# A two-layer hybrid encoder on one core: another order of the weight chunks, and wider matmuls in the up projection

## The chip, the core and the metric

The kernel runs on one core of one Trainium2 chip. The time is device microseconds of that core for one execution of the whole program; of several executions the median is taken. Five engines work beside each other, each through its own queue of instructions in a fixed order: TensorE (PE in the profile, its weight loads PEld), VectorE (DVE), ScalarE (ACT), GpSimd (POOL) and SyncE (SP, which here only issues transfers). An instruction that waits for another engine holds up all that stand behind it in its own queue.

## The reference

Input x is 256 rows of 1024 numbers, float32. Two layers are run. Each has a token-mixing part with three branches and a channel-mixing part:

```python
h = rms_norm(x, norm_mix_pre[i])
u_hy, q, k, v, g_out, gate_lr, u_pool, gate_logits = split(h @ w_in[i])
y_hy   = x0 * (fft_convolution(x1 * v_hy, filter) + bias * x1 * v_hy)  # x0, x1, v_hy: convolved thirds of u_hy
y_gla  = gated_linear_attention(q, k, v, g_out, gate_lr)              # 4 heads, both directions, chunks of 64 rows
y_pool = centred_mean_minus_self(u_pool, windows 2, 4, 8, 16) @ pool_w
gates  = sigmoid(gate_logits)                                         # 3 x 1024
merged = gates0 * (y_hy @ w_br_hyena) + gates1 * (y_gla @ w_br_gla) + gates2 * (y_pool @ w_br_pool)
x = x + rms_norm(merged @ w_out[i])
h = rms_norm(x, norm_ffn_pre[i])
a, b = split(h @ ffn_w_up[i], 2816)
x = x + rms_norm((gelu(dwconv3(a)) * b) @ ffn_w_down[i])
```

The decays of the attention are running sums of `max(log_sigmoid(gate) / 16, -1)` and enter as `exp` of them, so that logarithm, exponential, sigmoid, sine (in the filter) and GELU are all looked up in tables of ScalarE.

## The kernel before, in words

**Chunks.** All large weights of a layer are cut into 71 chunks of 128 x 2048 float32 (1 MB each), which SP fetches one after the other into three `raw` buffers. A chunk is then split into a high part in the matmul's reduced format (`split_upper`, line 205: one ACT copy of each half, 128 x 1024) and the low remainder (`split_lower`, line 222: one DVE subtraction of each half). Activations are kept as a high and a low part too. A product is three matmuls: high by high, high by low, low by high. Two ways to multiply are in use. In `chunk_x_stationary` (line 552) the activations are loaded as the stationary operand and 512 columns of weights move. In `ftile` (line 570) 128 columns of weights are stationary and the 256 rows of x move; `two_ftiles` (line 576) does so for the two halves of a 256-column chunk, with both results in one PSUM bank, and hands the bank to a function `post`.

**Order.** `CHUNK_ORDER` (line 47) says in which order the chunks are fetched, split and used. Its numbers, in words: 0 to 3 values and output gates of the attention; 4 to 9 the three inputs of the convolution (x1 and v first, then x0); 10, 11 queries; 12, 13 keys; 14, 15 inputs of the pooling; 16 to 21 sigmoid gates and projection of the convolution's branch (16, 17, 19, 20 gates, 18 and 21 projection); 22 to 27 the same for pooling; 28 to 33 for the attention; then output projection, up projection, down projection. A small chunk `lr` (the low-rank gate of the attention's decays) is put in after the fourth. In the kernel before, the order is values and gates, `lr` and decays, x1, v, x0, queries, pooling inputs, keys, and then the three branches (pooling, convolution, attention), each as gates and projection, half by half.

**Work beside the chunks.** `unit` (line 320) records the matmuls of a chunk and then lets side work go one step (`tick`) and splits later chunks ahead (`filler`), as far as `ahead["chunks"]` and the free buffers allow. Side work is written as generators: the convolution's filter (`filt`), the convolution (`hyena`), the pooling (`pool_pair`), the decays (`decay_gate`, four heads: two matmuls, two Exp on ACT, a minimum on DVE, one Ln on ACT, two scans on DVE, eight Exp of 128 x 128 on ACT), and the attention (`gla_head`). `post` of a query or key chunk multiplies the bank by the decays (`qk_post`, line 751), so that the bank stays taken until the decays are there. The program's own buffers are 37 slots of 4 KB per partition (`big`), 9 of 2 KB (`sml`) and 8 PSUM banks (`psm`); a slot goes to the next user in the order in which slots were given back.

**Who sets the order of instructions.** A scheduler that runs when the program is built puts the recorded instructions of each engine into their final order; the kernel steers it by the order of recording. Functions that need a table of ACT (Sin, Exp, Ln, Sigmoid, Gelu) keep their recorded order among themselves. Where two neighbours of these need different tables, a table load is put in front of the second. In the kernel before, `decay_all` (line 714) loads the set that has both logarithm and exponential, and all four heads run before the next sigmoid.

**Up projection.** For each of 11 pairs (order `UP_ORDER`), chunk a goes through `two_ftiles` and `a_post` (a three-tap convolution: one ACT and two DVE instructions for each 128 columns, then GELU); for 7 of the pairs chunk b goes through `two_ftiles` and `b_post`. That is 18 chunks of this kind a layer.

Of the kernel before, what the change touches and what calls it, by code (L numbers as in the profile page):

```python
# [18 lines left out]
P = 128  # L19
# [27 lines left out]
CHUNK_ORDER = (*range(12), 14, 15, 12, 13, *range(22, 28), *range(16, 22), *range(28, NCHUNK))  # L47
# [37 lines left out]
def trunk(ctx: ExitStack, tc: tile.TileContext, a: dict, out: bass.AP):  # L85
# [5 lines left out]
    big = Slots(spool, "b", 37, 4096)  # L91
# [3 lines left out]
    def f32(ap):  # L95
        return ap.bitcast(F32)
# [452 lines left out]
    def xt_alloc():  # L549
        return ([big.get([P, 4, L], F32R) for _ in range(2)], [big.get([P, 4, L], F32R) for _ in range(2)])  # L550
# [19 lines left out]
    def ftile(n, xt, f, o, width=256, kn=8):  # L570
        xth, xtl = xt
# [4 lines left out]
    def two_ftiles(n, xt, post):  # L576
# [14 lines left out]
    def layer(i, xt, chains):  # L591
# [13 lines left out]
        gw2 = big.get([P, DM])  # L605
        nc.gpsimd.dma_start(gw2[:], a["gw2"][i])
# [32 lines left out]


        nl = pos_of[("lr", i)]
        lrt = sml.get([P, L], F32R)
        pslr = psm.get([P, L])

        def fin_lr():
            act(lrt[:], pslr[:])
            tt(lrt[96:P, :], pslr[96:P, :], f32(lrt[96:P, :]), ALU.subtract)
            psm.put(pslr)

        def pe_lr():  # L650
            for k in range(8):
                w = wh[nl][0][:, k].rearrange("p a c -> p (a c)")
                for m in range(2):
                    mm(pslr[:], w, xt[m][k // 4][:, k % 4, :], k == 0 and m == 0, k == 7 and m == 1)

        ahead.update(chunks=3, reserve=0)
        unit([nl], pe_lr, fin_lr, cost=1.8, free=nl)
        g2 = room([P, DM], F32R)
        act(g2[:], gw2[:])
        tt(g2[32:64, :], gw2[32:64, :], f32(g2[32:64, :]), ALU.subtract)  # L660
        big.put(gw2)

        eb = [big.get([P, 2, 2, L]) for _ in range(2)]
        enb = [big.get([P, 2, 2, L]) for _ in range(2)]


        ebl = sml.get([P, 4, 3, 4])

        def rev(ap2):
            return bass.AP(ap2.tensor, ap2.offset + L - 1, [list(ap2.ap[0]), [-1, L]])  # L670

        ngb = cpool.tile([P, 8], F32, tag="ngb", name="ngb")
        nc.vector.tensor_scalar_mul(ngb[:], vec[:, i * NVEC + V_GB:i * NVEC + V_GB + 8], -1.0)

# [833 lines left out]
```

## Time and profile before

| | |
|---|---|
| median of 3 runs | 885.04 us (884.83 to 885.62) |
| the profiled execution's own time | 884.6 us |
| its span in the profile | 882.8 us |
| TensorE busy | 872.6 us, 99% |
| VectorE busy | 636.0 us, 72% |
| ScalarE busy | 512.4 us, 58% |
| table loads on ScalarE | 11, of 1283 ns each |
| mean granted clock of TensorE | 0.996 |

The 1.8 us between the profiled execution's time and its span lie outside of the first and the last instruction. A matmul's duration in the profile counts from its start to its last result, and the matmuls overlap; what one of them costs in a stream is the busy time of a group divided by its count. Layer 0 fills roughly the first 460 us of the span. Its mixing part ends at about 254 us, its up projection runs from about 265 to 392 us and its down projection follows. In the views, L120, L111, L106 and L114 are the lines of small helpers (matmul, DVE tensor-tensor, ACT, DVE scalar-tensor-tensor), so groups are told apart by tiles and shapes. Tile names are `b` for a 4 KB slot, `s` for a 2 KB slot, `p` for a PSUM bank, `raw` for a fetched chunk.

### The profile page before, as it was taken

How to read it: one execution, taken by the hardware profiler on the slowest of the kernel's cores; microseconds unless marked ns; L12 is line 12 of the kernel's file. 1: busy time of each engine (PE TensorE's matmuls, PEld its weight loads, DVE VectorE, ACT ScalarE, POOL GpSimd, SP SyncE). 2: the span in 40 equal slices, each digit the busy share in tenths (PEclk: the TensorE clock that was granted, in tenths of full speed). 3: DMA queues.
4: the chain of work that ended last, by engine and by line, in shares of the span. 5: the costliest groups of instructions: out<-in, count | busy, mean ns of one | idle time of the engine just before them, and what ended most of it. 6: DMA issues, size and time to landing. Idle time of an engine off the chain costs nothing.

```text
span 882.8 us, 13499 instructions
## 1 busy us (share of the span) xinstructions
PE 872.6 (99%) x5381; PEld 783.1 (89%) x5381; DVE 636.0 (72%) x925; ACT 512.4 (58%) x809; POOL 37.4 (4%) x86
## 2 busy tenths in 40 slices
PE   9999999999999999999999999999999999999997
PEld 7899987888888999998889999888888899999885
DVE  7899988766586798665288989876755967776612
ACT  7779666555365776554268865864543665555501
POOL 3000100000010000000010000000000000000000
PEclk9999999999999999999999999999999999999999
DMA  9854535746546446466349453465752674445501
GB/s 319 336 192 170 168 105 190 241 144 238 191 163 244 143 136 246 149 222 226 120 136 338 175 160 131 153 198 177 279 184 81 236 284 143 166 173 199 204 1 48
DMA packets 48431, 163.46 MB, mean 185 GB/s; under 512 B 3442, under 2 KB 29189, under 8 KB 33520
## 3 DMA queue, kind: packets, MB, share of 16 engines
q1 hardware_dynamic: 44352, 151.69, 49.2%
q0 software_dynamic: 4000, 10.90, 3.9%
q8 instruction: 42, 0.69, 0.3%
q14 instruction: 21, 0.17, 0.1%
q10 hardware_dynamic: 16, 0.00, 0.0%
HBM read 161.54 MB, written 1.05 MB: 184 GB/s over the span
## 4 chain that ended last, share of the span: by engine, by line
PE 96%; DVE 2%; DMA 1%; ACT 0%; issue 0%; SPq 0%; DVEq 0%; POOLq 0%; POOL 0%; ACTq 0%
PE p L120 94%; DVE b L111 1%; DMA raw<-in_wts 1%; PE p L374 1%; PE p L1059 0%; PE p L1204 0%; DMA x<-in_x 0%; ACT b L106 0%; PE p L775 0%; PE p L876 0%; PE p L1021 0%; DVE b L114 0%; DVE b L1281 0%; DVE s L111 0%; PE p L1294 0%
## 5 line engine op out<-in xcount | busy, mean ns | idle before, releaser
L120 PE MATMUL p<-b,b 128*128 128x256 f32 (+2 forms) x5022 | 842.1, 328 | 2.6 <-DVE b L111 1.9
L120 PEld LDWEIGHTS p<-b,b 128*128 128x128 f32 x5022 | 740.9, 190 | 85.6 <-DVE b L111 3.4
L111 DVE TENSOR_TENSOR b<-raw,b 128x1024 fp32r<-128x1024 f32 (+2 forms) x288 | 342.2, 1208 | 112.7 <-ACT b L106 55.2
L106 ACT ACTIVATE b<-raw 128x1024 fp32r<-128x1024 f32 (+2 forms) x290 | 292.0, 1041 | 159.3 <-PE p L120 128.3
L111 DVE TENSOR_TENSOR b<-p,b 128x512 f32<-128x512 f32 (+2 forms) x72 | 45.7, 654 | 66.5 <-ACT s L106 44.6
L106 ACT ACTIVATE b<-p 128x512 f32<-128x512 f32 (+3 forms) x90 | 50.1, 571 | 66.0 <-PE p L120 39.6
L106 ACT ACTIVATE s<-p 128x256 f32<-128x256 f32 (+3 forms) x50 | 20.3, 415 | 69.0 <-PE p L120 68.7
L114 DVE SCALAR_TENSOR_TENSOR s<-p,vec,s 128x255 f32<-128x255 f32 x104 | 49.3, 478 | 6.4 <-ACT s L106 5.5
L106 ACT ACTIVATE s<-p,vec 128x256 f32<-128x256 f32 x52 | 28.8, 558 | 19.0 <-DVE s L114 15.4
L106 ACT ACTIVATE s<-s 128x512 f32<-128x512 f32 (+6 forms) x54 | 29.0, 537 | 11.1 <-DVE s L111 5.6
L111 DVE TENSOR_TENSOR b<-s,b 128x512 fp32r<-128x512 f32 (+1 forms) x42 | 28.5, 685 | 6.0 <-ACT b L106 6.0
L106 ACT ACTIVATE b<-s 128x512 fp32r<-128x512 f32 x38 | 23.5, 625 | 9.6 <-DVE s L111 9.5
L111 DVE TENSOR_TENSOR b<-b,b 128x512 f32<-128x512 f32 (+4 forms) x28 | 22.4, 802 | 3.8 <-ACT b L106 3.3
L111 DVE TENSOR_TENSOR b<-b,p 128x512 f32<-128x512 f32 x24 | 16.2, 684 | 8.9 <-PE p L120 8.5
L111 DVE TENSOR_TENSOR s<-s,p 128x512 f32<-128x512 f32 x22 | 15.0, 683 | 8.1 <-ACT s L106 7.7
L106 ACT ACTIVATE b<-b,s 128x128 f32<-128x128 f32 x64 | 20.5, 395 | 0.0
L114 DVE SCALAR_TENSOR_TENSOR b<-p,vec,b 128x255 f32<-128x255 f32 (+1 forms) x40 | 19.1, 477 | 0.4 <-ACT b L106 0.3
L387 POOL TENSOR_TENSOR rstd<-mse,mhalf 128x1 f32<-128x1 f32 x16 | 8.9, 557 | 208.0 <-DVE mse L117 208.0
L106 ACT ACTIVATE b<-p,vec 128x256 f32<-128x256 f32 (+1 forms) x24 | 12.7, 530 | 8.1 <-PE p L120 5.8
L106 ACT ACTIVATE b<-b 1x512 f32<-1x512 f32 (+3 forms) x16 | 12.4, 780 | 4.1 <-DVE b L111 4.1
L106 ACT ACTIVATE s<-x 128x512 f32<-128x512 f32 x12 | 7.6, 633 | 11.6 <-DVE x L114 11.4
L164 POOL DMA_DIRECT2D b<-in_gains x7 | 3.9, 553 | 235.0 <-PE p L120 123.2
(108 smaller groups left out, 319.0 us busy)
## 6 DMA issues: line engine op xcount, KB each, us to landing
raw<-in_wts SPq DMA_DIRECT2D x116, 1024.0 KB, 4.9
raw<-in_wts SPq DMA_DIRECT2D x50, 512.0 KB, 4.7
b<-in_gains POOLq DMA_DIRECT2D x7, 512.0 KB, 4.9
b<-in_dft POOLq DMA_DIRECT2D x4, 512.0 KB, 5.4
raw<-in_wts SPq DMA_DIRECT2D x4, 256.0 KB, 5.4
b<-in_gw POOLq DMA_DIRECT2D x2, 512.0 KB, 6.1
b<-in_fw POOLq DMA_DIRECT2D x2, 512.0 KB, 7.3
b<-in_decay POOLq DMA_DIRECT2D x2, 512.0 KB, 7.6
```

Of the source, the lines that this page charges most:

```text
L106: ins = nc.scalar.activation(o, i, func, **kw)
L111: nc.vector.tensor_tensor(out=o, in0=x, in1=y, op=op)
L114: nc.vector.scalar_tensor_tensor(out=o, in0=x, scalar=s, in1=y, op0=op0, op1=op1)
L120: ins = nc.tensor.matmul(o, w, x, start=start, stop=stop).ins
L164: eng.dma_start(g[:], bass.AP(src.tensor, src.offset + (i * 4 + j) * DM, [[0, P], [1, DM]]))
L374: nc.tensor.transpose(ps[k // 4][:, k % 4, :], h[:, k * P:(k + 1) * P], ident[:])
L387: nc.gpsimd.tensor_tensor(out=r[:], in0=e[:], in1=mhalf[:, 0:1], op=ALU.pow)
```

## The change

Two things change. First, the chunks of the mixing part come in another order, and with it the parts of the program: values and gates, x1, v, x0, pooling inputs, the pooling branch (gates and projection), `lr`, then the decays beside the gates of the convolution's branch, queries and keys, the projection of the convolution's branch, and last the gates and the projection of the attention's branch. `branch` is cut into `gates` and `project`; the gates of a branch are held in buffers until its projection. How far splits run ahead of use changes too: 5 chunks with 3 slots kept in reserve where the convolution's inputs start, against 3 and 0 before.

Second, the high and the low part of an activation tile stand next to each other in memory (two fixed tiles for a layer's input in place of four `big` slots, of which there are now 33). In the up projection one matmul then moves 512 columns, 256 of the high and 256 of the low part, past the high weights; a second moves the 256 high columns past the low weights. Each 128 columns of output take a whole PSUM bank, whose two halves are added afterwards (one ACT copy, one DVE addition), and `post` reads the sum from a 2 KB slot.

```diff
-CHUNK_ORDER = (*range(12), 14, 15, 12, 13, *range(22, 28), *range(16, 22), *range(28, NCHUNK))
+CHUNK_ORDER = (*range(10), 14, 15, 22, 23, 25, 26, 24, 27, 16, 17, 19, 20, *range(10, 14), 18, 21, 28, 29, 31, 32, 30, 33,
+               *range(34, NCHUNK))
+LR_AT = 18
...
-    big = Slots(spool, "b", 37, 4096)
+    big = Slots(spool, "b", 33, 4096)
...
-        order.insert(len(order) - NCHUNK + 4, ("lr", i))
+        order.insert(len(order) - NCHUNK + LR_AT, ("lr", i))
...
     def xt_alloc():
-        return ([big.get([P, 4, L], F32R) for _ in range(2)], [big.get([P, 4, L], F32R) for _ in range(2)])
+        ts = [cpool.tile([P, 4, 2, L], F32R, tag=f"xt{j}", name=f"xt{j}") for j in range(2)]
+        return ([t[:, :, 0, :] for t in ts], [t[:, :, 1, :] for t in ts], ts)
...
+    def ftiles_wide(n, xt, banks, lows):
+        for f, o in enumerate(banks):
+            for k in range(8):
+                h, l = weights(n, k * 256 + f * P, P)
+                x = xt[2][k // 4][:, k % 4]
+                if lows:
+                    mm(o[:, 0, :], l, x[:, 0, :], False, k == 7)
+                else:
+                    mm(o[:], h, x, k == 0, False)
...
+    def two_ftiles(n, xt, post, wide=False):
+        if wide:
...
+            tmp = sml.get([P, 2, L])
+            banks = [psm.get([P, 2, L]) for _ in range(2)]
+            def out():
+                for f, ps in enumerate(banks):
+                    act(tmp[:, f, :], ps[:, 1, :])
+                    tt(tmp[:, f, :], tmp[:, f, :], ps[:, 0, :], ALU.add)
+                psm.put(*banks)
+                post(tmp)
+                sml.put(tmp)
+            unit([n], lambda: ftiles_wide(n, xt, banks, False), cost=3.6)
+            unit([n], lambda: ftiles_wide(n, xt, banks, True), out, cost=1.9, free=n)
+            return
...
         two_ftiles(take(), xt, pool_post(0))
+        handles["x0"] = True
         two_ftiles(take(), xt, pool_post(2))
...
+        gates(0)
+        drain(*pool_h)
+        project(0, y_pl)
...
+        unit([nl], pe_lr, fin_lr, cost=1.8, free=nl)
...
+        f_dec = start(decay_all())
...
+        gates(1)
+        drain(f_dec, *gates_ready)
...
+        two_ftiles(take(), xt, qk_post(eb, 0, float(P ** -0.5)))
+        two_ftiles(take(), xt, qk_post(eb, 1, float(P ** -0.5)))
+        for pair in range(2):
+            two_ftiles(take(), xt, qk_post(enb, pair, None))
+        f_gla = start(gla())
+        drain(f_hy)
+        project(1, handles["y_hy"])
...
+        gates(2)
+        drain(f_gla)
+        project(2, (y_gl["h"], y_gl["l"]))
...
-            two_ftiles(take(), xt2, a_post)
+            two_ftiles(take(), xt2, a_post, True)
             if pair >= NB:
-                two_ftiles(take(), xt2, b_post)
+                two_ftiles(take(), xt2, b_post, True)
```

What the built programs show of this, at three places.

On TensorE, the start of a chunk of the up projection in layer 0 before (`b3` and `b29` are the low-numbered slots that hold the high and the low part of x, `b32` and `b15` high and low weights):

```order
L120 MATMUL p4_115_2939<-b3_225_2476,b32_249_2707 128x256
L120 MATMUL p4_115_2939<-b29_227_2478,b32_249_2707 128x256
L120 MATMUL p4_115_2939<-b3_225_2476,b15_250_2708 128x256
L120 MATMUL p4_115_2939<-b3_225_2476,b32_249_2707 128x256
L120 MATMUL p4_115_2939<-b29_227_2478,b32_249_2707 128x256
L120 MATMUL p4_115_2939<-b3_225_2476,b15_250_2708 128x256
```

And a whole chunk of the same stage now (`xt0` and `xt1` hold both parts of x, `b2` and `b4` are high weights, `b25` and `b27` low ones):

```order
L123 MATMUL p0_118_2973<-xt0_2466,b2_245_2779 128x512 x4
L123 MATMUL p0_118_2973<-xt1_2467,b4_256_2830 128x512 x4
L123 MATMUL p2_119_2974<-xt0_2466,b2_245_2779 128x512 x4
L123 MATMUL p2_119_2974<-xt1_2467,b4_256_2830 128x512 x4
L123 MATMUL p0_118_2973<-xt0_2466,b25_246_2780 128x256 x4
L123 MATMUL p0_118_2973<-xt1_2467,b27_257_2831 128x256 x4
L123 MATMUL p2_119_2974<-xt0_2466,b25_246_2780 128x256 x4
L123 MATMUL p2_119_2974<-xt1_2467,b27_257_2831 128x256 x4
```

Three matmuls of 256 columns have become one of 512 and one of 256; a chunk has 32 in place of 48, takes two banks, and needs its low weights only after its high ones. Over both layers there are 576 matmuls fewer.

On ScalarE, the decays of the first two heads in layer 0 before (`s2` and `s8` hold one head's gate each, `b51`, `b70` and the like are splits and the convolution's work):

```order
L106 ACTIVATE s2_13_681<-p0_23_642,ngb_448 128x256 x2
L106 ACTIVATE b20_51_452<-p3_20_603,vec_69 128x256
L106 ACTIVATE s2_13_681<-s2_13_681 128x512
L106 ACTIVATE s8_14_739<-p5_24_686,ngb_448 128x256 x2
L106 ACTIVATE b27_76_921<-raw12_601 128x1024
L106 ACTIVATE s4_11_670<-s1_2_356 1x512
L106 ACTIVATE s8_14_739<-s8_14_739 128x512
```

And the same two heads now, with the sigmoid of the convolution's gates (`b10_136`) among them:

```order
L109 ACT_TABLE_LOAD
L109 ACTIVATE s0_38_1540<-p2_56_1517,ngb_1471 128x256 x2
L109 ACTIVATE b13_127_1431<-b12_44_421 128x512
L109 ACTIVATE b3_143_1575<-raw24_1442 128x1024
L109 ACT_TABLE_LOAD
L109 ACTIVATE s0_38_1540<-s0_38_1540 128x512
L109 ACT_TABLE_LOAD
L109 ACTIVATE s1_39_1563<-p3_58_1545,ngb_1471 128x256 x2
L109 ACTIVATE b28_148_1623<-raw25_1524 128x1024
L109 ACTIVATE b27_150_1714<-raw25_1524 128x1024
L109 ACT_TABLE_LOAD
L109 ACTIVATE s1_39_1563<-s1_39_1563 128x512
```

Each step from Exp to Ln, from Ln to Exp and from either to a sigmoid now has a table load in front. The whole program has 37 of them, against 11.

On ScalarE, two neighbouring sigmoids of the convolution's gates in layer 0 before (`b36_159`; `raw` rows are splits, `s8` and `s4` belong to the attention's heads):

```order
L106 ACTIVATE b36_159_1831<-p0_63_1832 128x512
L106 ACTIVATE b20_157_1825<-raw26_1749 128x1024
L106 ACTIVATE s8_43_1896<-p1_64_1874 128x2x128
L106 ACTIVATE s8_43_1896<-p5_65_1875 128x256
L106 ACTIVATE s4_50_2104<-b18_50_446,s6_7_447 128x128 x2
L106 ACTIVATE b27_166_1926<-raw28_1829 128x1024
L106 ACTIVATE b26_168_1963<-raw28_1829 128x1024
L106 ACTIVATE b36_159_1831<-p4_66_1882 128x512
```

And the last decays with the last of these sigmoids now (`b31`, `b2` are decays of heads 2 and 3, `b0_145` is the second half of the gates, whose last bank is `p0_62`):

```order
L109 ACTIVATE s3_42_2033<-b17_134_1468,s8_37_1470 128x128
L109 ACTIVATE s5_44_2112<-b17_134_1468,s8_37_1470 128x128
L109 ACTIVATE b31_133_1467<-b2_135_1469,s8_37_1470 128x128 x4
L109 ACTIVATE b2_135_1469<-b2_135_1469,s8_37_1470 128x128 x4
L109 ACTIVATE s8_37_1470<-s8_37_1470 128x2
L109 ACT_TABLE_LOAD
L109 ACTIVATE b0_145_1581<-p0_62_1661 128x512
```

Before, splits and a few copies stand between the sigmoids. Now the sigmoid that empties bank `p0_62` stands behind the decays of all four heads. On TensorE the next user of that bank is the fourth matmul group of the convolution's projection, `p0_70`; the pieces of TensorE's queue between them are 48 matmuls for each of four query and key chunks and three groups of 12.

More of the change, by code (lines that the diff above doesn't have):

```diff
@@ L570, in ftile @@
     def ftile(n, xt, f, o, width=256, kn=8):
[L571 removed]
+        xth, xtl = xt[:2]
         for k in range(kn):
@@ L637, in layer @@
             big.put(g_cur.pop("pre"))
[L641 to L670, printed above, removed]
@@ L712, in layer @@
-        gates_ready = []
-        def decay_all():
-            while not kfs[i].get("sines"):
-                yield
-            ld = nc.scalar.preload_act_table_set("natural_log_exp_and_others")
-            tc.stamp_issue_order_token(ld.ins, TOKEN)
-            for h in range(4):
-                gates_ready.append(start(decay_gate(h)))
-                yield
-        flush()
-        f_dec = start(decay_all())
+        ahead.update(chunks=5, reserve=3)
         zv = big.get([P, 4, L])
@@ L1064, in merge_up, with gates @@
                 big.put(merged[half])
-        def branch(b, ready):
+        def gates(b):
+            if b == 2:
+                ahead.update(chunks=7, reserve=4)
             for half in range(2):
                 gate = room([P, 2, 512])
+                gated[b, half] = gate
                 if b == 0:
@@ L1080, in branch, with project @@
                              post if j else None, free=nj if t else None)
-                ys = ready()
+            if b == 2:
+                flush()
+        def project(b, ys):
+            for half in range(2):
+                gate = gated.pop((b, half))
                 n = take()
-                if b == 2 and half == 1:
-                    flush()
-                    big.put(*xt[0], *xt[1])
                 if b == 2:
@@ new lines, in layer, with rev @@
+        ahead.update(chunks=3, reserve=0)
+        unit([nl], pe_lr, fin_lr, cost=1.8, free=nl)
+        g2 = room([P, DM], F32R)
+        act(g2[:], gw2[:])
+        tt(g2[32:64, :], gw2[32:64, :], f32(g2[32:64, :]), ALU.subtract)
+        big.put(gw2)
+        eb = [big.get([P, 2, 2, L]) for _ in range(2)]
+        enb = [big.get([P, 2, 2, L]) for _ in range(2)]
+        ebl = sml.get([P, 4, 3, 4])
+        def rev(ap2):
+            return bass.AP(ap2.tensor, ap2.offset + L - 1, [list(ap2.ap[0]), [-1, L]])
@@ new lines, in layer, with decay_all, qk_post, post @@
+        gates_ready = []
+        def decay_all():
+            while not kfs[i].get("sines"):
+                yield
+            ld = nc.scalar.preload_act_table_set("natural_log_exp_and_others")
+            tc.stamp_issue_order_token(ld.ins, TOKEN)
+            for h in range(4):
+                gates_ready.append(start(decay_gate(h)))
+                yield
+        flush()
+        f_dec = start(decay_all())
+        def qk_post(dst, pair, scale):
+            def post(ps):
+                for z in range(2):
+                    d = dst[pair][:, :, z, :]
+                    if scale is None:
+                        tt(d, ps[:], d, ALU.mult)
+                    else:
+                        stt(d, ps[:], scale, d)
+            return post
```

142 lines of the change are left out of this document (66 added, 76 removed).

## The prediction

> **What bounds the kernel now.** I read the page first, then TensorE's waits, then its groups in a quiet stretch, and last the busy time by stage. The page shows one engine that is nearly never free:
>
> ```profile
> span 882.8 us, 13499 instructions
> PE 872.6 (99%) x5381; PEld 783.1 (89%) x5381; DVE 636.0 (72%) x925; ACT 512.4 (58%) x809; POOL 37.4 (4%) x86
> PE 96%; DVE 2%; DMA 1%; ACT 0%; issue 0%; SPq 0%; DVEq 0%; POOLq 0%; POOL 0%; ACTq 0%
> ```
>
> TensorE works 872.6 of 882.8 us, and 96% of the chain that ended last is TensorE. All that it ever waited for, over the whole program, is this:
>
> ```profile
> PE p L120 <- DVE b L111: 1.9, 2, 1.8
> PE p L120 <- DVE rmask L260: 1.2, 1, 1.2
> PE p L120 <- ACT b L106: 0.6, 1, 0.6
> ```
>
> The 1.8 us is the one stall inside the program. So the time changes by what leaves TensorE's stream, and by waits that are new. What a matmul costs in a stream without stalls is read from the end of the last up projection with the down projection (771 to 876 us), where both forms run:
>
> ```profile
> L120 PE MATMUL p<-b,b 128*128 128x512 f32 x263 | 59.8, 389 | 0.0
> L120 PE MATMUL p<-b,b 128*128 128x256 f32 x381 | 45.9, 283 | 0.0
> ```
>
> Busy time by count: 59.8 / 263 = 0.2274 us for 512 columns, 45.9 / 381 = 0.1205 us for 256. Twice 256 columns cost 0.2410, which is 0.0135 more than 512 at once: each matmul carries a fixed cost of about that size beside its columns.
>
> **The change part by part.** *Wide matmuls.* For each 128 output columns and each k, three matmuls of 256 columns (3 x 0.1205 = 0.3615) become one of 512 and one of 256 (0.2274 + 0.1205 = 0.3479), 0.0135 less (unrounded). There are 18 chunks x 2 x 8 = 288 such groups a layer, 576 in all: 576 x 0.0135 = **7.8 us** off TensorE's stream. The sum rests on the row of 512 holding where x moves in place of weights: both are 512 neighbouring float32 of one partition into a whole bank. The ends of this cost are 0 (columns alone count) and 7.8; I take 7.8, since both rows stand for hundreds of matmuls.
>
> A rule of the Trainium skill speaks against that size: the page "TensorE: Matmul & The Clock Gate", section "Back-to-back issue gap", gives N / 2.4 + 2.5 ns, a fixed part of 2.5 ns; the saving would then be 576 x 2.5 ns = 1.4 us (an estimate from that page). This trace disagrees: the same two rows give a fixed part of 13.5 ns.
>
> *The stall that may go.* At 132 us of layer 0 TensorE waited for a low part of a chunk:
>
> ```profile
> 133.00 1.22 DVE L111 TENSOR_TENSOR b<-raw,b 128x1024 fp32r<-128x1024 f32 x1
> ...
> 134.28 6.02 PE L120 MATMUL p<-b,b 128*128 128x512 f32 x18 [1.76 <-DVE b L111]
> ```
>
> The stages around it (columns: window, its length, busy us and count of PE, PEld, DVE, ACT, POOL, granted clock, DMA share, GB/s):
>
> ```profile
> 75.00:115.00 40.00, 40.00 (x318) 38.87 (x317) 37.80 (x71) 28.78 (x61) 3.84 (x13) 1.00 0.51 163
> 115.00:132.00 17.00, 17.00 (x82) 14.24 (x81) 14.17 (x20) 11.36 (x18) 0.00 (x0) 1.00 0.37 125
> ...
> 134.30:139.00 4.70, 4.70 (x14) 3.69 (x15) 4.69 (x9) 2.23 (x5) 0.00 (x0) 0.64 0.68 209
> ```
>
> DVE worked 51.97 of the 57 us ahead of the stall. After it the granted clock fell to 0.64 over 4.7 us, which costs 0.36 x 4.7 = 1.7 us more: 1.76 + 1.7 = **3.5 us** in all. In the new order the decays and the query and key chunks come behind the pooling branch. What that takes from DVE ahead of the place where pooling and convolution meet is, from these rows, eight scans (0.68 each), eight half-bank operations (0.42 each) and eight products with the decays (0.68 each) of one layer, and a split of 1.2 us:
>
> ```profile
> L111 DVE TENSOR_TENSOR b<-raw,b 128x1024 fp32r<-128x1024 f32 x282 | 338.6, 1221 | 111.5 <-PE p L120 54.5 <-ACT b L106 54.0 <-issue 2.0
> L111 DVE TENSOR_TENSOR b<-b,p 128x512 f32<-128x512 f32 x24 | 16.2, 684 | 8.9 <-PE p L120 8.5
> L691 DVE TENSOR_TENSOR_SCAN b<-rmask,s 128x256 f32<-128x256 f32 x8 | 5.4, 681 | 0.0
> L686 DVE TENSOR_SCALAR s<-s 128x512 f32<-128x512 f32 x8 | 3.3, 417 | 0.0
> ```
>
> That is 5.4 + 3.3 + 5.4 + 1.2 = 15.3 us of DVE work moved behind, against a stall of 1.8. I take the stall and its slow clock as gone: -3.5 us; the other end is 0 (another stall in its place).
>
> *Table loads.* The change has 26 loads more (37 against 11), 33 us of ACT, nearly all among the decays. ACT has room over the program (512 of 883 us), so what counts is the stretch from the first sigmoid of the convolution's gates to the last, which empties the bank that TensorE needs for the last 12 matmuls of the convolution's projection. The rows:
>
> ```profile
> L106 ACT ACTIVATE b<-raw 128x1024 fp32r<-128x1024 f32 x282 | 287.9, 1054 | 157.9 <-PE p L120 128.3 <-DMA raw<-in_wts 23.5 <-DVE b L111 2.2
> L106 ACT ACTIVATE b<-p 128x512 f32<-128x512 f32 x54 | 31.8, 588 | 39.8 <-PE p L120 39.6
> L106 ACT ACTIVATE b<-b,s 128x128 f32<-128x128 f32 x64 | 20.5, 395 | 0.0
> L106 ACT ACTIVATE s<-s 128x512 f32<-128x512 f32 x30 | 18.7, 624 | 5.4 <-DVE s L114 4.4 <-DVE s L686 0.8
> L106 ACT ACT_TABLE_LOAD x9 | 11.5, 1283 | 1.5 <-PEq L1498 1.4
> L106 ACT ACTIVATE s<-p,ngb 128x256 f32<-128x256 f32 x16 | 6.6, 469 | 0.0
> ```
>
> Busy by count gives 1.02 for a split, 0.59 for a sigmoid or a copy from PSUM, 0.32 for an Exp of 128 x 128, 0.62 for a Ln, 0.41 for an Exp of a gate, 1.28 for a load. Layer 0 has in that stretch 12 loads (15.4), 16 splits or copies of that size (16.4), 6 sigmoids and copies (3.5), 2 half splits (1.2), 8 gate Exp (3.3), 4 Ln (2.5), 36 small ones (11.5) and four tiny ones (0.8): 54.6 us. TensorE's own work over the same stretch is 118 matmuls of 512 columns (26.8), 200 of 256 (24.1) and 8 transposes (about 1): 51.9. ACT is late by about 2.7 us. In layer 1 there are 11 splits and 32 small ones and no copies: 15.4 + 11.2 + 2.4 + 3.3 + 2.5 + 10.2 + 0.8 = 45.8, against 99 and 200 matmuls, 22.5 + 24.1 = 46.6; it ends just in time. I take **+2.5 us**. The lower end is 0: operations in a full queue overlap a little, and the sum of layer 0 shrinks below TensorE's. The upper end is all 26 loads on the path, +33 us. Behind the late sigmoid stand the splits of the chunks of the attention's gates; they are needed some 3 us and more after the place where TensorE waits, so they are late next only if ACT is late by more than that.
>
> The Trainium skill, page "ScalarE: Activation LUTs", section "Table sets: the hidden batching unit", advises to batch calls by set and names a set that holds both Exp and Ln, so it, too, speaks against this order.
>
> *Adding the two halves.* Each wide chunk adds two ACT copies and two DVE additions of 128 x 256, and takes two of the eight PSUM banks in place of one. From the nearest rows they cost 0.38 and 0.42 each, while the four DVE taps of an `a` chunk read a 2 KB slot in place of PSUM, at 0.42 in place of 0.48:
>
> ```profile
> L106 ACT ACTIVATE s<-p 128x256 f32<-128x256 f32 x16 | 5.8, 384 | 3.8 <-PE p L120 3.6
> L111 DVE TENSOR_TENSOR b<-p,b 128x256 fp32r<-128x256 f32 x8 | 3.4, 420 | 5.4 <-ACT b L106 5.4
> L114 DVE SCALAR_TENSOR_TENSOR s<-p,vec,s 128x255 f32<-128x255 f32 x104 | 49.3, 478 | 6.4 <-ACT s L106 5.5
> L114 DVE SCALAR_TENSOR_TENSOR s<-b,b 128x256 f32<-128x256 f32 x8 | 3.1, 418 | 0.0
> ```
>
> The narrowest place is the first half of layer 0's up projection, where the filter of layer 1 is made as well:
>
> ```profile
> 286.00:345.00 59.00, 59.00 (x469) 57.20 (x468) 52.27 (x80) 42.55 (x61) 0.52 (x1) 1.00 0.49 175
> 345.00:449.00 104.00, 104.00 (x646) 94.10 (x645) 58.20 (x71) 47.85 (x62) 2.74 (x5) 1.00 0.48 170
> ```
>
> About nine chunks run in the 59 us: DVE gets 18 x 0.42 = 7.6 more and 24 x 0.06 = 1.4 less, so 58.5, while TensorE's share shrinks by 9 x 16 x 0.0135 = 1.9 to 57.1. DVE is over by 1.4 us; the chunks split ahead cover that, and the next stretch leaves 46 us free. The filter takes four banks at a time there, which leaves room for two wide chunks. I take **+0.5 us**, between 0 and 4: should a wide chunk have to wait for its banks each time that the filter holds four (two or three times), each wait is at most a chunk's own two copies and two additions, 1.6 us.
>
> *The rest at nothing.* The later `lr` and its two transfers, the order of fetching and the gate buffers add no instruction; the small transfer has the two pooling projections in front of its use (48 matmuls of 0.2274, 10.9 us), and costs its landing time if they did not cover it.
>
> *Sum.* 884.6 - 7.8 - 3.5 + 2.5 + 0.5 = 876.3 against the profiled execution's own time; the median of the runs shown is 885.04, 0.4 above it, so **876.7 us**.
>
> **The rivals.** *Columns alone count, or the wide form does not do what it says.* If a matmul that moves x at 512 columns costs twice one of 256, nothing leaves the stream: 884.6 - 3.5 + 2.5 + 0.5 + 0.4 = 884.5, no change. Against it stand the two rows of 263 and 381; for it, that no 512-column matmul of before moves x. Chance 0.06. By the fixed part that the Trainium skill's section on the issue gap gives, it would be 1.4 less, 883.1; the trace bears that out no better.
>
> *ACT's queue decides (slower).* In the decays ACT hands over to DVE and back three times a head, 24 times in all, and each time now waits in order, with nothing to spare in either layer. A row for such a handover:
>
> ```profile
> ACT s L106 <- DVE s L114: 19.8, 20, 2.3
> ```
>
> One wait is 1.0 us on average, 2.3 at worst. With 1.0 at each, 24 us come on top: 876.7 + 24 = about 900. It decides as soon as the mean wait passes 8.3 / 24 = 0.35 us. Against it: the load in front of a Ln (1.28) hides the minimum on DVE (0.42), and the scans have another head's work and two splits to hide behind. Chance 0.10, with 0.07 of it slower and 0.03 at no change.
>
> *The up projection stalls.* Banks or DVE hold TensorE up there by 4 us in place of 0.5: 880.2. For it, the 89% of DVE in the 59 us and the doubled banks; against it, the next stretch. Chance 0.12, still faster.
>
> *The attention's heads end late.* From the first head's scores to the last head's transposes TensorE had 179 matmuls of 512 columns beside them before (40.7 us at 0.2274), in layer 0; now it has 120 (27.3), since only the last gates and a part of the projection are left. That is 13.4 us less cover a layer. If a quarter of it is missed, each layer loses 3.4 us: 883.5. For it, the heads are chains over four engines; against it, there is no wait of TensorE at all in that place before, so that some of the 40.7 was spare. Chance 0.06, half of it still faster.
>
> **How the numbers follow.** The forecast has 0.62, with a range of its own from 873.7 (no new cost) to 880. Something better than it, with other small waits gone, has 0.04. Differences within 0.2% (883.3 to 886.8) can't be told from no change. Faster: 0.62 + 0.04 + 0.12 + 0.03 and 0.01 of the first rival, 0.82. Same: 0.05 of the first rival, 0.03 of the second and 0.03 of the last, 0.11; slower: 0.07. The range from 872.5 to 882.7 holds the forecast, what is better by up to 1 us, the stalled up projection, and half of the last rival; about 0.17 lies above it and 0.02 below.
>
> **What would show it.** The 512-column group grows from 2040 to 2616 and the 256-column group falls from 2912 to 1760, at 0.227 and 0.120 us each in the up projection; any other price there breaks the first term. The list of TensorE's waits should have lost the 1.8 us on a low part near 132 us, and the clock should stay at 1.00 there. A wait on ACT of some 2 us should appear about 60 us behind `lr` in layer 0, ahead of the last group of the convolution's projection, and none or a small one in layer 1; waits there of over 5 us would mean that the table loads decide. DVE should be above 95% in the first half of layer 0's up projection, with TensorE waiting little. The prediction is wrong if the time is above 883.

## The result: slower by 2.7%, and the profile after

The changed kernel takes 908.12 us (median of 4, 907.36 to 910.25) against 884.93 for the kernel before, measured beside it: a ratio of 1.0269, with a 95% interval from 1.0249 to 1.0289. The prediction was 876.7. So some 23 us are lost where 8 were to be gained, and 31 us have to be explained.

The head of the page of the changed kernel, and its chain of waits by engine:

```profile
span 906.7 us, 12484 instructions
PE 882.6 (97%) x4805; PEld 758.2 (84%) x4805; DVE 660.7 (73%) x997; ACT 569.2 (63%) x907; POOL 37.2 (4%) x86
PE 82%; ACT 10%; DVE 4%; issue 2%; DMA 1%; SPq 0%; DVEq 0%; POOLq 0%; ACTq 0%
```

TensorE's share of the chain fell from 96% to 82%, and ScalarE's rose from 0% to 10%. TensorE has 576 matmuls fewer and is nevertheless busy 10 us longer. Its waits (who waited for whom, us in total, times, longest):

```profile
PE p L123 <- DVE s L928: 5.9, 2, 5.1
PE p L989 <- DVE b L114: 5.0, 2, 2.5
PE p L123 <- ACT b L109: 4.2, 2, 3.2
PE p L123 <- DVE rmask L263: 1.2, 1, 1.2
PE p L123 <- DVE b L114: 0.7, 2, 0.3
PE p L1337 <- DVE b L1332: 0.4, 1, 0.4
```

That is 17.4 us in place of 3.7. Three places are new: the last sigmoid of the convolution's gates (ACT, layer 0), the select of an attention head (L928, layer 1 above all), and the transposes of the merged halves (L989, 2.5 us in both layers). By time (window, length, busy us and count of PE, PEld, DVE, ACT, POOL, granted clock, DMA share, GB/s):

```profile
130.00:140.00 10.00, 10.00 (x49) 8.32 (x48) 5.44 (x7) 6.48 (x9) 0.00 (x0) 1.00 0.31 105
...
150.00:160.00 10.00, 10.00 (x70) 9.27 (x70) 7.91 (x14) 9.91 (x16) 0.00 (x0) 1.00 0.67 241
160.00:170.00 10.00, 10.00 (x85) 10.00 (x85) 6.21 (x9) 9.94 (x18) 0.00 (x0) 1.00 0.62 204
170.00:180.00 10.00, 10.00 (x71) 9.39 (x70) 8.40 (x17) 9.91 (x16) 0.00 (x0) 1.00 0.63 189
180.00:190.00 10.00, 6.80 (x29) 5.24 (x28) 5.71 (x14) 9.98 (x27) 0.00 (x0) 0.97 0.07 23
190.00:200.00 10.00, 10.00 (x45) 8.31 (x44) 10.00 (x15) 6.61 (x10) 0.56 (x1) 0.86 0.63 216
...
620.00:630.00 10.00, 10.00 (x51) 8.47 (x50) 7.51 (x14) 9.94 (x25) 0.00 (x0) 1.00 0.34 107
630.00:640.00 10.00, 10.00 (x51) 8.37 (x50) 9.97 (x14) 4.86 (x7) 0.00 (x0) 1.00 0.50 173
640.00:650.00 10.00, 4.93 (x26) 4.40 (x25) 8.57 (x12) 7.38 (x13) 0.00 (x0) 0.84 0.58 197
```

Where the old stall stood (about 132 us) TensorE is full and the clock is 1.00. From 150 to 190 us, in the decays, ACT has no free moment; when it comes out of that, DVE is full in its place (190 to 200, 630 to 640). And behind each of the four longer waits of this execution the granted clock falls. Shorter windows of the same kernel:

```profile
188.00:192.00 4.00, 4.00 (x12) 3.12 (x13) 3.16 (x4) 4.00 (x6) 0.00 (x0) 0.67 0.02 4
...
648.00:652.00 4.00, 4.00 (x17) 3.79 (x17) 1.83 (x5) 1.37 (x7) 0.72 (x1) 0.50 0.97 317
```

In these two windows alone 0.33 x 4 = 1.3 us and 0.50 x 4 = 2.0 us of TensorE's work are lost while it counts as busy.

The place of the wait in layer 1, in the timeline of the changed kernel (start, us, engine and operation):

```profile
641.77 0.83 PE L123 MATMUL p<-b,b 128*128 128x128 f32 x6
647.67 2.05 PE L123 MATMUL p<-b,s 128*128 128x128 f32 x8 [5.07 <-DVE s L928]
```

```profile
643.30 0.48 DVE L911 TENSOR_SCALAR s<-b,s 128x128 f32<-128x128 f32 x2
643.69 3.49 DVE L114 TENSOR_TENSOR b<-raw,b 128x1024 fp32r<-128x1024 f32 x3
647.09 0.43 DVE L928 COPY_PREDICATED s<-pmask,p 128x256 f32<-128x256 uint8 x1
```

The head's scores are through TensorE at 642.6. Its select on DVE (0.43 us) stands in the queue behind three low parts of weight chunks, 3.49 us. DVE had had next to no free moment since 630 us (9.97 of 10 in the window from there), so the low parts had piled up in its queue.

### The profile page after: what moved, and what is told of

Same layout as the page of the kernel before. It is cut to its first block, busy times and chain, and to the rows that moved or that the text cites. A ratio compares the mean times of both kernels' runs of the same rounds, so it can differ in the third digit from the quotient of the medians.

```text
span 906.7 us, 12484 instructions
## 1 busy us (share of the span) xinstructions
PE 882.6 (97%) x4805; PEld 758.2 (84%) x4805; DVE 660.7 (73%) x997; ACT 569.2 (63%) x907; POOL 37.2 (4%) x86
## 4 chain that ended last, share of the span: by engine, by line
PE 82%; ACT 10%; DVE 4%; issue 2%; DMA 1%; SPq 0%; DVEq 0%; POOLq 0%; ACTq 0%
PE p L123 80%; ACT b L109 6%; DVE b L114 4%; ACT L109 3%; ACT s L109 1%; DMA x<-in_x 1%; DMA raw<-in_wts 1%; PE p L989 1%; PE p L377 1%; PE p L1248 0%; PE p L716 0%; PE p L953 0%; PE p L817 0%; PE p L1337 0%; SPq L202 0%
## 5 line engine op out<-in xcount | busy, mean ns | idle before, releaser
L114 DVE TENSOR_TENSOR b<-raw,b 128x1024 fp32r<-128x1024 f32 (+1 forms) x288 | 343.6, 1209 | 95.4 <-ACT b L109 64.6
L109 ACT ACTIVATE b<-raw 128x1024 fp32r<-128x1024 f32 (+1 forms) x290 | 292.6, 1040 | 128.0 <-PE p L123 83.0
L123 PE MATMUL p<-xt,b 128*128 128x256 f32 (+1 forms) x2336 | 353.8, 310 | 0.0
L123 PEld LDWEIGHTS p<-xt,b 128*128 128x128 f32 x2336 | 323.6, 188 | 29.2 <-issue 0.7
L123 PE MATMUL p<-b,b 128*128 128x512 f32 (+1 forms) x1150 | 269.7, 389 | 3.9 <-ACT b L109 3.2
L123 PEld LDWEIGHTS p<-b,b 128*128 128x128 f32 x1150 | 211.3, 190 | 47.4 <-ACT b L109 3.9
L123 PE MATMUL p<-b,xt 128*128 128x512 f32 x960 | 236.5, 400 | 1.0 <-ACT b L109 1.0
L123 PEld LDWEIGHTS p<-b,xt 128*128 128x128 f32 x960 | 179.1, 190 | 44.1 <-ACT b L109 1.3
L117 DVE SCALAR_TENSOR_TENSOR s<-s,vec,s 128x255 f32<-128x255 f32 x88 | 40.0, 482 | 5.3 <-ACT s L109 4.9
L114 DVE TENSOR_TENSOR s<-s,p 128x256 f32<-128x256 f32 (+1 forms) x80 | 33.9, 445 | 4.6 <-ACT s L109 4.5
L109 ACT ACTIVATE b<-s 128x512 fp32r<-128x512 f32 x38 | 23.1, 624 | 10.9 <-DVE s L114 10.8
```

The lines of the kernel that those rows point to most:

```text
L109: ins = nc.scalar.activation(o, i, func, **kw)
L114: nc.vector.tensor_tensor(out=o, in0=x, in1=y, op=op)
L117: nc.vector.scalar_tensor_tensor(out=o, in0=x, scalar=s, in1=y, op0=op0, op1=op1)
L123: ins = nc.tensor.matmul(o, w, x, start=start, stop=stop).ins
```

## The experiments

All kernels below were timed beside the kernel before (883.9 to 885.1 us in these measurements); ratios are to it.

### 1 to 4: the two halves of the change, and the place of x

The order alone keeps x in large slots and the up projection narrow:

```diff
-        two_ftiles(take(), xt2, a_post, True)
+        two_ftiles(take(), xt2, a_post)
-        ts = [cpool.tile([P, 4, 2, L], F32R, tag=f"xt{j}", name=f"xt{j}") for j in range(2)]
+        # two big slots each for the high and the low parts; big has 37 slots
```

> The new order of chunks and steps alone: both parts of x lie in two separate buffers of the large slots again (37 slots), and every matmul that moves x has 256 columns, as before the change. Theory A (the loss of the changed kernel has two sources: new waits of TensorE in the decays, the attention's heads and the last projection, about 22 us with the slow clock behind them, and slower reads of x in its new place, about 11 us; the wide matmuls and the old stall give back 7.8 and 3.5): 884.9 - 3.5 + 22 = 903.5 us, with TensorE's waits on ACT, on L989's transposes and on the heads still there, and matmuls at 0.227 and 0.120 us. Rival B (the new order costs little, the wide form and the smaller number of slots cost the time): 881 to 886 us.

Measured: 910.78 us, ratio 1.0291 [1.0261, 1.0321]. So the order alone is slower by some 26 us, and rival B is out. It is 7 us more than theory A said; its profile has the same waits, a little longer.

The wide matmuls alone: the order, the steps and `branch` of the kernel before, with the change's `xt_alloc`, `ftiles_wide` and `two_ftiles`.

> The wide matmuls alone, in the old order: x in the two fixed buffers of the change (33 large slots), which start 32 bytes behind a multiple of 64. Theory A: -7.8 for the wide form, +3.8 because a matmul that moves 512 columns of x takes 0.234 in place of 0.227 us, +6.7 because 960 matmuls with x as the stationary operand take 0.234 in place of 0.227: 884.9 + 2.7 = 887.6 us, with the stall at 132 us still there. Rival B (the wide form itself is what costs): 900 us and more. The prediction's first step: 884.9 - 7.8 + 0.5 = 877.6 us.

Measured: 885.94 us, ratio 1.0018 [1.0005, 1.0032]. No gain, as theory A said, and no loss from the wide form either. Why it gains nothing came from the addresses: the two fixed tiles of x start at bytes 31200 and 39392 of a partition, odd multiples of 32; all large slots, in both kernels, start at multiples of 128. So both were moved by 32 bytes:

```diff
-    fw2 = cpool.tile([64, DEPTH * P], F32, name="fw2")
+    fw2 = cpool.tile([64, DEPTH * P + 8], F32, name="fw2")[:, 0:DEPTH * P]
-        ngb = cpool.tile([P, 8], F32, tag="ngb", name="ngb")
+        ngb = cpool.tile([P, 32], F32, tag="ngb", name="ngb")[:, 0:8]
```

(`fw2` lies ahead of x; the second line keeps the slots, from which the weights are read, on multiples of 128. They move by 128 bytes, to a start of 75264 in place of 75136, so that the distance from x to a slot changes too.)

> As the wide matmuls alone in the old order, but both fixed buffers of x start 32 bytes later, on a multiple of 128 bytes, as the large slots do. Theory A1 (the place of x in its partition decides how fast TensorE reads it): 512 columns at 0.227 us in all groups, so 884.9 - 7.8 + 0.5 = 877.6 us, some 10 us below the kernel with the buffers 32 bytes earlier. Rival A2 (the place does not matter; a moving or stationary operand is slower because both parts of x lie beside each other in one buffer, or because of the fixed buffers): the same time as with the buffers 32 bytes earlier, about 887.6 us.

Measured: 878.14 us, ratio 0.9930 [0.9905, 0.9956]: 7.8 us better by 32 bytes. The same in the changed kernel:

> The changed kernel whole, with both buffers of x 32 bytes later, on a multiple of 128 bytes. Theory A1 (place): 908.1 - 10.5 = 897.6 us, with 512 columns at 0.227 us in every group and the new waits of TensorE as they were. Rival A2 (the place does not matter): 908 us.

Measured: 900.85 us, ratio 1.0188 [1.0152, 1.0225], 7.3 better than the changed kernel, where theory A1 had named 10.5. So the place of x counts in both, and rival A2 is out. A1 took it for x's own address; experiment 11 shows below that it is not. Groups of TensorE by shape, of the old order with wide matmuls, first with x on an odd multiple of 32 bytes:

```profile
L120 PE MATMUL p<-b,xt 128*128 128x512 f32 x960 | 236.3, 399 | 2.6 <-DVE b L111 1.6 <-ACT b L106 1.0
L120 PE MATMUL p<-xt,b 128*128 128x256 f32 x1760 | 225.1, 282 | 0.0
L120 PE MATMUL p<-xt,b 128*128 128x512 f32 x576 | 142.1, 396 | 0.0
```

then on a multiple of 128:

```profile
L120 PE MATMUL p<-b,xt 128*128 128x512 f32 x960 | 231.6, 394 | 3.1 <-DVE b L111 1.7 <-ACT b L106 1.4
L120 PE MATMUL p<-xt,b 128*128 128x256 f32 x1760 | 224.9, 283 | 0.0
L120 PE MATMUL p<-xt,b 128*128 128x512 f32 x576 | 139.4, 392 | 0.0
```

The 960 matmuls that hold x as the stationary operand cost 4.7 us more at the first place, and the 576 wide ones 2.7 more: 7.4 us, 5 ns a matmul, for nothing but a place in memory.

### 5, 6, 8: what in the order costs the time

All three start from the changed kernel with x on a multiple of 128 bytes (900.85 us). Without the table loads:

```diff
-                        act(gate[:, t, :], ps[:], AF.Sigmoid)
+                        act(gate[:, t, :], ps[:], AF.Copy if b == 1 else AF.Sigmoid)
```

> The changed kernel with x on a multiple of 128 bytes (900.85 us), with the sigmoid of the convolution's gates left out: a plain copy of the same size stands in its place, so that no table has to be loaded between these gates and the decays' Exp and Ln. Theory T (the loads, 1.28 us each, make ACT late): TensorE's wait on ACT near 184 us (3.6 us) and the slow clock behind it (about 1.7 us) go, and the first head of layer 1 comes earlier too: 900.85 - 5.3 = 895.5 us or less. Rival Q (what counts is that the decays and the heads have too little TensorE work beside them, and ACT's and DVE's queues are full of splits; the loads fill gaps): the waits stay and the time is 899 to 901 us.

Measured: 886.01 us, ratio 1.0009 [0.9994, 1.0025]: 14.8 us better, 2.8 times the 5.3 that theory T named. Table loads on ACT, of the changed kernel and then of this one (two more stand on a line of their own in each):

```profile
L109 ACT ACT_TABLE_LOAD x35 | 44.9, 1283 | 2.1 <-PEq L1541 1.4 <-PE p L123 0.2
```

```profile
L109 ACT ACT_TABLE_LOAD x11 | 14.1, 1283 | 1.7 <-PEq L1541 1.4 <-PE p L123 0.2
```

But two things were left out at once. A sigmoid keeps its recorded place among the Exp and Ln of the decays, and a plain copy does not, so the scheduler put the copies further ahead. The last one of layer 0, which empties the bank that the projection needs, in the kernel with the sigmoid and then in this one:

```profile
186.38 0.60 ACT L109 ACTIVATE b<-p 128x512 f32<-128x512 f32 x1
```

```profile
155.95 0.58 ACT L109 ACTIVATE b<-p 128x512 f32<-128x512 f32 x1
```

It comes 30 us earlier, and the layer's 12 loads of 1.28 us are only 15.4 of that: it no longer stands behind the decays of all four heads, but among those of the first. So the 14.8 us belong to the loads and to the place of these sigmoids together, and this run does not part them. With the two the wait on ACT in layer 0 goes, and so does the wait for the head in layer 1, which names DVE. What stays of TensorE's waits is almost only L989:

```profile
PE p L989 <- DVE b L114: 5.0, 2, 2.5
PE p L123 <- DVE rmask L263: 1.2, 1, 1.2
PE p L123 <- ACT b L109: 1.0, 1, 1.0
PE p L123 <- DVE b L114: 0.9, 3, 0.3
```

The attention's branch half by half:

```diff
-        gates(2)
+        gates(2, (0,))
         drain(f_gla)
-        project(2, (y_gl["h"], y_gl["l"]))
+        project(2, (y_gl["h"], y_gl["l"]), (0,))
+        gates(2, (1,))
+        project(2, (y_gl["h"], y_gl["l"]), (1,))
```

> The changed kernel with x on a multiple of 128 bytes (900.85 us), with the attention's branch half by half as before the change: gates of half 0, projection of half 0, gates of half 1, projection of half 1. Theory M (the waits of 2.5 us at L989 arise because all four sums of the last projection close at once behind the last head, and the transposes of the merged halves then stand behind four products and four sums on DVE; each costs a slow clock of about 1.7 us besides): both waits go, 900.85 - 2 x (2.7 + 1.7) = 892 us. Rival H (the heads are late anyway, and the gates of half 1, 32 matmuls or 7.3 us a layer, were their cover): the wait moves ahead of the projection of half 0, and the time is 899 us or more.

Measured: 900.28 us, ratio 1.0166 [1.0140, 1.0192]. No gain: rival H. The waits at L989 went and others came, on ACT, in this kernel's list:

```profile
PE p L122 <- ACT b L108: 8.1, 4, 3.5
PE p L122 <- DVE s L927: 5.9, 1, 5.9
```

The decays earlier:

```diff
         gates(0)
+        # lr, its fetch (LR_AT = 16) and the start of the decays stand here
         drain(*pool_h)
         project(0, y_pl)
-        # ... and no longer here
         gates(1)
```

> The changed kernel with x on a multiple of 128 bytes (900.85 us), with one thing moved: lr and the decays start behind the gates of pooling in place of behind the projection of pooling, so that 48 matmuls of 512 columns (10.9 us of TensorE) more stand beside the decays. All table loads, gates and projections stay. Theory Q (too little work beside the decays): the wait on ACT near 184 us goes (-5.3 with its slow clock), and the wait for the first head in layer 1 (6.2 us and some 2.5 of slow clock) goes for the most part: 887 to 892 us, the two waits at L989 left. Rival T (the table loads fill ACT's queue wherever the decays stand): less than 3 us better, 898 to 901 us.

Measured: 885.77 us, ratio 1.0012 [0.9999, 1.0025]: 15.1 us better, and nothing is left out. But it does not tell Q from T, since the projection of pooling has no sigmoid, and with it beside the decays the number of table loads falls as well, from 37 to 17.

### 7, 10, 11: the two causes together, and loads against cover

> The changed kernel with x on a multiple of 128 bytes, the sigmoid of the convolution's gates left out (a copy in its place; 886.01 us with that alone, 13 table loads in place of 37) and the attention's branch half by half. Theory M2 (with heads that come in time, the closing of all four sums at once is what costs the two waits of 2.5 us at L989; half by half it goes, and the earlier test of it failed only because the heads were late): 886.0 - 2 x (2.7 + 1.7) = 877.2 us. Rival H2 (the gates of half 1 are needed as the heads' cover even so): a wait ahead of the projection of half 0 takes its place, 884 us or more.

Measured: 881.63 us, ratio 0.9960 [0.9944, 0.9975], between the two theories.

> The changed kernel with x on a multiple of 128 bytes, lr and the decays behind the gates of pooling (885.77 us with that alone, 17 table loads) and the attention's branch half by half; nothing is left out. Theory M2: the two waits at L989 go, and the two of 1.1 us behind them: 885.8 - 2 x (2.7 + 1.3) = 877.8 us, about the time of the old order with wide matmuls and x on a multiple of 128 bytes (878.14). Rival H2: the heads wait in place of it, 884 us or more.

Measured: 878.68 us, ratio 0.9927 [0.9911, 0.9942]. With heads that come in time the half-by-half branch is worth 4.4 and 7.1 us, against 8.8 and 8.0 expected by theory M2: the second run bears it out, the first by half. TensorE's waits of the second of these kernels, complete:

```profile
PE p L122 <- ACT b L108: 2.2, 2, 1.1
PE p L122 <- DVE rmask L262: 1.2, 1, 1.2
PE p L122 <- DVE mse L119: 1.1, 1, 1.1
PE p L122 <- DVE s L927: 0.8, 1, 0.8
```

Loads put back by hand where the decays start early:

```diff
+        dum = cpool.tile([P, 32], F32, tag="dum", name="dum")
...
+            act(dum[:, h:h + 1], ngb[:, h:h + 1], AF.Sigmoid)
             act(t[:], t[:], AF.Ln, bias=1.0)
```

> The kernel with lr and the decays behind the gates of pooling (885.77 us, 17 table loads) with 24 table loads more: a sigmoid of one column ahead of each head's Ln (and one more in one head) makes ACT load the sigmoid's table and then the decays' table again. The work beside the decays is as in that kernel. It tells whether the loads cost by themselves or only where too little TensorE work stands beside them. Theory T (each load lengthens the decays, which are late wherever they stand): the 24 loads take 30.8 us of ACT and about half of that comes on top, as in the changed kernel (15 us): 895 to 901 us. Theory Q (the 10.9 us more of TensorE work hide them): 886 to 890 us.

Measured: 907.98 us, ratio 1.0259 [1.0242, 1.0275]: 22.2 us more for 24 loads, in spite of 10.9 us more of TensorE work beside the decays. Theory Q falls: the loads cost by themselves, with all other work on ACT in the same order in layer 0 and nearly so in layer 1. In its windows ACT is full again and TensorE stands:

```profile
150.00:160.00 10.00, 5.63 (x29) 4.24 (x27) 4.96 (x11) 9.94 (x21) 0.00 (x0) 1.00 0.00 0
160.00:170.00 10.00, 8.59 (x50) 8.59 (x51) 6.43 (x10) 9.93 (x18) 0.00 (x0) 0.66 0.74 285
```

The 22.2 us are not all loads, though. Matmuls with x have become dearer too, those of the up projection among them, where none of the 24 loads stands. First without the 24 loads, then with them:

```profile
L123 PE MATMUL p<-b,xt 128*128 128x512 f32 x960 | 228.4, 393 | 2.0 <-ACT b L109 2.0
L123 PE MATMUL p<-xt,b 128*128 128x512 f32 x576 | 139.4, 392 | 0.0
```

```profile
L123 PE MATMUL p<-b,xt 128*128 128x512 f32 x960 | 232.5, 397 | 1.0 <-ACT b L109 1.0
L123 PE MATMUL p<-xt,b 128*128 128x512 f32 x576 | 141.8, 396 | 0.0
```

The buffer `dum` of the small sigmoids takes 128 bytes behind x, and all slots move by them (to a start of 75392, from 75264); x stays at 31232, a multiple of 128. So a change of the distance between x and the weights by 128 bytes is enough, and x's own address is not what sets the price. These two groups cost 4.1 + 2.4 = 6.5 us more. An estimate from them leaves some 15 to 16 us for the 24 loads: about half of their 30.8 us of ACT, near the upper end of theory T and near the 14.8 us above.

### 9 and 12: the old stall, and another place

Pooling ahead of the queries and keys in the old order with wide matmuls:

```diff
-CHUNK_ORDER = (*range(12), 14, 15, 12, 13,
+CHUNK_ORDER = (*range(10), 14, 15, 10, 11, 12, 13,
```

> The wide matmuls in the old order with x on a multiple of 128 bytes (878.14 us), with one step of the new order: the two chunks of pooling go ahead of the first two chunks of queries and keys. Everything else stands as in the old order. If the stall at 132 us (a low part, late on DVE) comes from the products of queries and keys ahead of it, it goes with its slow clock: 878.1 - 3.5 = 874.6 us. Rival: another low part is late instead, or the attention's heads come later and TensorE waits there: 878 us or more.

Measured: 879.82 us, ratio 0.9935 [0.9914, 0.9955]. The rival: TensorE still waits there, now for a high part on ACT (1.7 us at the most). So moving the products of two chunks of queries and keys is not enough to remove the stall. The 3.5 us that were to be gained were also too many here: the kernel without this step waits 1.7 us at that place, but its granted clock behind the wait is 1.00, against 0.83 for the same window of the kernel before.

> The wide matmuls in the old order once more, with both buffers of x 96 bytes behind their place in the change: on an odd multiple of 64 bytes. On a multiple of 128 it took 878.14 us, on an odd multiple of 32 it took 885.94. Theory A64 (a multiple of 64 bytes is enough): 878 us, with 512 columns at 0.227 us. Rival A128 (only a multiple of 128 gives the full speed, as all other operands lie on one in all kernels so far): 886 us, or in between if the slow-down goes by the part of the accesses that cross a line.

Measured: 877.83 us, ratio 0.9925 [0.9909, 0.9942]. The time is that of a multiple of 128, as A64 said, but not for the reason that it gave:

```profile
L120 PE MATMUL p<-b,xt 128*128 128x512 f32 x960 | 236.0, 398 | 2.3 <-DVE b L111 2.0 <-ACT b L106 0.3
L120 PE MATMUL p<-xt,b 128*128 128x256 f32 x1760 | 220.0, 279 | 0.0
L120 PE MATMUL p<-xt,b 128*128 128x512 f32 x576 | 140.0, 393 | 0.0
```

The stationary group is as slow as at 32 bytes, and the 256-column group is faster by 4.9 us than at either other place. The three groups add up to 603.5, 596.0 and 595.9 us for 32, 64 and 128; the times go with the sums. (The names of the places are those of x alone. In the 128 case the slots of the weights have the same remainder by 512 as x; in the 64 and 32 cases x starts 64 and 96 bytes behind theirs.)

### The way from before to after

| kernel | us | step |
|---|---|---|
| before | 884.9 | |
| wide matmuls, old order, x on a multiple of 128 | 878.14 | -6.8 |
| the new order, decays early, last branch half by half | 878.68 | +0.5 |
| the last branch's gates first, both projections behind the last head | 885.77 | +7.1 |
| the decays behind pooling's projection, 37 loads in place of 17 | 900.85 | +15.1 |
| x on an odd multiple of 32 (the changed kernel) | 908.12 | +7.3 |

The kernel before varied from 883.9 to 885.1 between these measurements, so each step is good to about 1 us (the first is -6.2 by the ratio of its own measurement). The order without its two faults is worth nothing here beyond that. Three kernels near 878 beat both kernels of the change by 0.7% and more; the simplest is the old order with the wide form and x moved by 32 bytes.

## Why the prediction was wrong, step by step

**Wide matmuls (-7.8).** The mechanism held. With x well placed the wide form with the added halves measured -6.2 (0.9930 of 884.9), where the prediction had -7.8 + 0.5. The Trainium skill's fixed part of 2.5 ns ("TensorE: Matmul & The Clock Gate", "Back-to-back issue gap", where it is the gap of an isolated matmul) would have given an estimate of -1.4 + 0.5 = -0.9 us. The interval of that run ends at 0.9956, which is -3.9 us: the trace disagrees with the page here too, and the 13.5 ns of the two rows stand. What failed is the sentence that the row of 512 holds "where x moves in place of weights": it did not hold at the place at which the change puts x (142.1 against 139.4 us), and the reason is not that x moves: where x is stationary the price rises as well.

**The stall that may go (-3.5).** It went: no wait on a low part of 1.8 us is left, and the clock is 1.00 from 130 to 140 us. Its working is not confirmed: moving pooling ahead of the queries and keys alone did not remove it. Half of the 3.5 was the slow clock behind it, and that part was not sure: the wide kernels of the old order keep a stall of 1.6 to 1.7 us there, and the clock behind it is 1.00 in all three. And the saving was lost in the new stalls.

**Table loads (+2.5, upper end 33).** This is the term that failed most. The loads, with the gates' sigmoids that keep their place among the decays, cost 14.8 us, and 24 loads alone some 15 to 16 at the other place. The wait that it forecast came where it was said and about as long (3.2 us against 2.7 in layer 0, none on ACT in layer 1). Its own sign, a wait of over 5 us there if the loads decide, did not come, and they decided all the same. Two things were left out. The first is the slow clock behind a wait, which the step before had counted as a gain and which this step did not count as a loss. The second is what is late next. The text asked it of the splits "needed some 3 us and more after the place", and did not follow the chain from the late Exp to the products of queries and keys on DVE, and from there to the first head. In layer 1 ACT "ends just in time", but ACT is full up to 630 us (9.94 of 10 in the last window), and DVE, which is free in part up to there (7.51), is full from 630 on. The head's select stands behind three low parts: 5.1 us of wait and a clock of 0.50. With the loads gone, and the sigmoids no longer held in place, this wait, on another engine, is gone too. That the late work on ACT is what fills DVE is the likely chain; the runs show its two ends. The page "ScalarE: Activation LUTs" of the Trainium skill ("Table sets: the hidden batching unit") had the right sign: batch by set.

**Adding the two halves (+0.5).** No run parts this cost from the wide form's gain. In the up projection of layer 0 DVE is full, as said, and TensorE never waits:

```profile
320.00:330.00 10.00, 10.00 (x56) 8.63 (x55) 10.00 (x20) 8.14 (x14) 0.00 (x0) 1.00 0.30 107
330.00:340.00 10.00, 10.00 (x56) 8.28 (x55) 10.00 (x18) 8.87 (x14) 0.00 (x0) 1.00 0.60 211
```

**The rest at nothing.** Two costs were in it. The new place of x to the weights also slows the 960 matmuls that hold x as stationary operand, an operand that the change was not thought to touch (4.7 of the 7.4 us). And the last branch: before, the gates of half 1 stood between the two projections. Now the four sums of both halves close at once behind the last head, and TensorE, at its transposes, waits for four products and the first of the sums with the other branches on DVE, 2.5 us in each layer: 4.4 to 7.1 us by the two runs that leave it out. The prediction knew the new order of this branch and gave these transposes no price.

**The rivals.** "ACT's queue decides" named about 900 us with a chance of 0.10, and with x well placed the kernel takes 900.85. That the two figures meet is luck. Its engine was right, its mechanism was not: it priced 24 waits at handovers, while ACT, at 9.9 of 10 us busy, waits for nothing; it is full. "The attention's heads end late" came true in layer 1 (5.1 us and its clock against 3.4), but not for want of matmuls beside them, as it had it: with the same order of chunks, and the loads and the place of the sigmoids changed, there is no wait at L928. "The wide form does not do what it says" and "the up projection stalls" did not come.

**What stays open.** The order alone is 26 us slower, the order on top of the wide form 22.7; of the 3 us between them TensorE's waits on ACT show most (7.1 us in the first, 3.9 in the second), and why they are longer is not shown. In the changed kernel itself the loads and the place of the sigmoids are not parted. And how the place of two operands makes a matmul dearer is not shown, only that it does.

## What to carry to other kernels

Before an order is changed, write down for each engine the sequence of its function tables and the share of its time in the stretch: where ACT had no free moment, about half of the loads' time was paid by the program, and the wait can show up on another engine, so follow the late result to each queue that it enters. A slow clock can stand behind a wait of TensorE; price it as a range, from nothing to the wait once more, since not every wait had one. When a buffer that TensorE reads gets a new home, look at its byte address within the partition, and at that of the other operand, before anything else. A projection whose sums all close at the same moment leaves the next step with nothing to hide behind; keep a half back.

## What the runs showed of the hardware that was not expected

The place of a matmul's two operands to each other sets its price. Moving both tiles of x by 32 bytes, and the slots by 128, changed the whole program by 7.8 and 7.3 us (two pairs of kernels). By groups: with x stationary and 512 columns of weights moving, 960 matmuls took 231.6 us with x on a multiple of 128 bytes, 236.0 and 236.3 on odd multiples of 64 and 32; with 256 columns of x moving, 1760 took 224.9, 220.0 and 225.1; with 512 columns of x moving, 576 took 139.4, 140.0 and 142.1. It is not x's own address that counts: with the 24 loads put back, x lies where it lay before, all slots are 128 bytes further on, still on multiples of 128, and the 576 take 141.8 us. Nor is it the slots' own address. In that kernel the matmuls of the down projection (in the window from 770 to 876 us) have two slots as operands, and their row reads:

```profile
L123 PE MATMUL p<-b,b 128*128 128x512 f32 x162 | 36.9, 389 | 0.0
```

Two slots still cost 0.228 us a matmul, against the 0.227 of before. In all kernels at the lower price x and the slots have the same remainder by 512; at 64, 96 and 128 bytes off it some group or other was dearer. Other distances were not tried.

And not every wait of TensorE has a slow clock behind it. The changed kernel had one behind each of its waits of 2.5 us at L989. With the decays started early the same two waits of 2.5 us are there, and the clock stays at 1.00 behind both; layer 0:

```profile
230.00:240.00 10.00, 6.36 (x33) 4.38 (x32) 8.82 (x13) 5.35 (x7) 1.12 (x2) 1.00 0.54 194
240.00:250.00 10.00, 10.00 (x45) 8.26 (x44) 1.43 (x3) 1.32 (x4) 0.00 (x0) 1.00 0.23 95
```
